# Product-key expert layer and two blocks on one core: dense expert activations for two token tiles instead of three, one tile with gathered u rows, one tile with gathered u and v rows that joins the second block last

## The chip, the cores and the metric

The kernel runs on one core of a Trainium2 chip. The metric is the device time of one execution in microseconds; the kernel before took 2317.34 us (median of three runs, 2315.11 to 2320.51).

## The reference

512 tokens of width 1024 pass through two blocks. The first block has sliding-window attention and a pooling mixer, and then an expert layer with product keys: each token picks, in each of 8 heads, 16 of 16,384 experts. A picked expert has a row in `u_experts` and one in `v_experts`, each of 1024 values. The second block has dilated attention, spatial gating and a gated feed-forward layer. Cut to the expert layer and its surroundings:

```python
def peer(xn, w_query, sub_keys, u_tab, v_tab):      # xn: normed tokens
    def chunk(xc):                                   # 128 tokens
        ...
        sv, si = lax.top_k(sc, PEER_TOPK)            # per head and half: 16 of 128 keys
        ...
        fv, fi = lax.top_k(cand, PEER_TOPK)          # 16 of the 256 pairs
        idx = jnp.take_along_axis(cidx, fi, axis=-1)
        g = jax.nn.softmax(fv, axis=-1)
        u = u_tab[idx]
        a = jax.nn.gelu(jnp.einsum('chkd,cd->chk', u, xc), approximate=False)
        vv = v_tab[idx]
        return jnp.einsum('chk,chkd->cd', (g * a), vv)
...
h = h + peer(rmsnorm(h, ln_ffn_g[l]), ...)
return rmsnorm(h, ln_final_g)                        # then the second block
```

## The kernel before, in words

The 512 tokens are four tiles of 128 (tile 0 to 3). A float32 product is made of three matmuls on split operands (`mm3`, L135): high by high, high by low, low by high. Weights come as 512 KB loads into `wraw` (SyncE's queue), ScalarE copies the high part (`whi`, L130) and VectorE subtracts for the low part (`wlo`, L132).

The expert layer has two ways to serve a tile. **Gathered**: for each of a token's 128 picks an indirect DMA on GpSimd's queue fetches one row per token (128 rows, 512 KB) into one of four `gu` buffers (pool `gt`); for u, VectorE multiplies by the tokens and sums (L466); for v, VectorE adds the scaled row to the residual `hres` (L475). That is 256 gathers for a tile. **Dense**: all 16,384 experts meet the tile on TensorE, in 128 blocks of 128 experts. The activations of a block are 24 matmuls (tile `hps`) over the columns of the dense tiles, then Gelu to `hg`; they are multiplied by a gate matrix that is zero where a token did not pick the expert (`hw`), split (`hh`, `hl`) and multiplied by the block's 128 rows of v, 18 matmuls into six PSUM banks (`acc`). Before, tile 0 is gathered and tiles 1 to 3 are dense, so `hps` has 384 columns (`TD`).

The gate matrix of a tile is built in 8 groups of 16 tokens (`gate_matrix`): VectorE makes `oj` (L596) and part of the `og` (L606), ScalarE the other part (L609, L610), TensorE multiplies them (`wps`, L612), ScalarE copies to `stg` (L614), and 1 MB goes to DRAM. `decode` turns a tile's top-k results into gates and indices, on VectorE. Since the routing leaves TensorE free, `hps` blocks are computed there and **parked** in DRAM: 68 of 128 (`NPARK`), 16 of them beside the queries, the rest by `PARKS` behind each group of the gate matrix. `GATH` sets the gathers per group.

Three lists in the code set the order: within the routing and the second block a scheduler orders each engine's instructions by data and by the order of the code; the dense loop over 128 blocks is written by hand (`manual_schedule`, L695 on): it loads v three blocks ahead, splits two ahead, makes `hw` one ahead, and issues 0.9 gathers a block while activations are parked and 2.5 where they aren't (`RATE`). Engines take their instructions strictly in order, so a VectorE instruction that waits for a gather holds up all behind it.

The second block begins with the last norm of all four tiles and a transposition (`to_feature`), then `token_major` runs `w_in_2` in five column blocks over the four tiles, each weight pair serving all tiles; attention goes by tile (`scores`, `values`) in between.

Of the kernel before, what the change touches and what calls it, by code (L numbers as in the profile page):

```python
# [41 lines left out]
def body(ctx: ExitStack, tc: tile.TileContext, A: dict, out: bass.AP):  # L42
# [31 lines left out]
    def rstd_newton(var, which):  # L74
        """1 / sqrt(var + eps) by three Newton steps from the exponent-halving guess, on the vector engine alone."""
# [24 lines left out]
    def first_half(junk_pool, y):  # L100
        """mean square of a row's first half, halved, plus the norm's eps"""
# [23 lines left out]
    def wload(src, shape):  # L125
# [3 lines left out]
        hi = pool.tile(shape, F32R, name="whi", tag="whi")  # L129
        SC.activation(hi, raw, AF.Copy)  # L130
        lo = pool.tile(shape, F32R, name="wlo", tag="wlo")
# [23 lines left out]
    def halves(mm_pool, srcs, xh, xl, fill, parts=(0, 1)):  # L155
        """The blocks of srcs, two token tiles ahead of the other two; fill() readies those."""
        ws = [wload(src, [128, ND, 128]) for src in srcs]
        pss = [mm_pool.tile([128, S], F32, name="mm", tag="mm") for _ in srcs]
        for part in parts:
            sl = slice(part * 256, part * 256 + 256)  # L160
            if part == parts[1]:
                fill()
# [29 lines left out]
    # ------------------------------------------------ first block: mixers  # L192
# [203 lines left out]
    # ------------------------------------------------ product-key experts  # L396
    # token tile 0 gathers its expert rows; the other tiles meet every expert on the tensor engine
    with ExitStack() as st:
# [4 lines left out]
        gt = st.enter_context(tc.tile_pool(name="gt", bufs=4, reuse_waits="tile"))  # L403
# [3 lines left out]
        TD = S - 128  # L407
        TG = 16
# [688 lines left out]
```

## Time and profile before

| | us |
|---|---|
| median of three runs | 2317.34 |
| span of the profiled execution | 2313.5 |
| queries and top-k, 16 parked blocks (382 to 568.6 of the span) | 186.6 |
| gate matrices, 52 parked blocks, about 59 gathers (568.6 to 897) | 328.4 |
| dense loop (897 to 1690) | 793.0 |
| second block up to its feed-forward part (1690 to 1937) | 247.0 |
| the rest of the second block (1937 to 2313.5) | 376.5 |

The stages follow each other, so a stage's length is its share of the time. In each, the engines' busy times and the busy share of the 16 DMA engines tell which resource has no room left. The busy time of TensorE counts overlapping matmuls; what one costs in a row of its like is the distance between starts.

### The profile page before, as it was taken

The page shows a single profiled execution, that of the slowest core. Times are in us where ns is not written, and L with a number is a line of the kernel's source. Part 1 is how long each engine was busy: PE and PEld are TensorE (multiplying, and loading weights), DVE is VectorE, ACT ScalarE, POOL GpSimd, SP SyncE. Part 2 cuts the span into 40 slices and gives each one's busy share as a digit, 9 for nine tenths or more (in the row PEclk, how much of TensorE's full clock was granted, in tenths as well). Part 3 has the DMA queues.
Part 4 walks back from the last instruction along what each step waited for, and adds up shares of the span by engine and source line. Part 5 has one row for each costly group of instructions (what it writes and reads, how often), then busy time and mean ns, then how long its engine had stood idle before and what let it go on. Part 6 is the DMA issues. An engine that isn't in the chain of part 4 may idle for free.

```text
span 2313.5 us, 30184 instructions
## 1 busy us (share of the span) xinstructions
PE 2246.8 (97%) x11337; PEld 1931.4 (83%) x11337; DVE 1495.2 (65%) x2998; ACT 986.1 (43%) x1631; POOL 382.4 (17%) x261
## 2 busy tenths in 40 slices
PE   7999998999899999999999999999999999999998
PEld 6768887989799999777779999999976778888886
DVE  4553254989999994767777777777784555333323
ACT  4354233333897783333333333333353364322222
POOL 0000000000222430323323444444400000000000
PEclk9999999999899999999999999999999999999999
DMA  5202232443577997889899898889732112333331
GB/s 173 92 19 75 90 111 84 128 125 118 213 272 289 363 350 253 295 311 329 293 323 322 306 320 297 296 302 323 274 113 74 56 55 87 105 101 93 98 100 65
DMA packets 177572, 444.82 MB, mean 192 GB/s; under 512 B 15249, under 2 KB 84241, under 8 KB 174353
## 3 DMA queue, kind: packets, MB, share of 16 engines
q1 hardware_dynamic: 140560, 308.65, 39.8%
q0 software_dynamic: 36864, 134.23, 16.3%
q8 instruction: 89, 1.46, 0.2%
q14 instruction: 59, 0.48, 0.1%
HBM read 402.19 MB, written 40.63 MB: 191 GB/s over the span
## 4 chain that ended last, share of the span: by engine, by line
PE 86%; DVE 5%; ACT 4%; DMA 4%; issue 1%; DVEq 0%; ACTq 0%; SPq 0%
PE mm L136 13%; PE mm L137 12%; PE mm L138 12%; PE hps L138 7%; PE hps L136 7%; PE hps L137 7%; PE acc L136 6%; PE acc L138 6%; PE acc L137 6%; DMA wraw<-in_v_experts_dram 3%; PE wps L612 2%; PE sc L311 1%; PE pv L346 1%; ACT stg L614 1%; PE sc L889 1%
## 5 line engine op out<-in xcount | busy, mean ns | idle before, releaser
L130 ACT ACTIVATE whi<-wraw 128x1024 fp32r<-128x1024 f32 x232 | 241.8, 1045 | 568.9 <-PE mm L137 343.0
L132 DVE TENSOR_TENSOR wlo<-wraw,whi 128x1024 fp32r<-128x1024 f32 x232 | 278.7, 1204 | 265.9 <-ACT whi L130 261.5
L136 PE MATMUL hps<-x2h,whi 128*128 128x384 f32 x1024 | 348.1, 340 | 2.1 <-ACT whi L130 1.8
L138 PE MATMUL hps<-x2h,wlo 128*128 128x384 f32 x1024 | 345.1, 337 | 0.8 <-DVE wlo L132 0.8
L137 PE MATMUL hps<-x2l,whi 128*128 128x384 f32 x1024 | 344.2, 336 | 0.0
L464 POOL DMA_INDIRECT gu<-in_u_experts_dram,ix x128 | 190.8, 1491 | 914.0 <-PE wps L612 605.5
L136 PE MATMUL acc<-whi,hh 128*128 128x512 f32 x768 | 302.6, 394 | 17.3 <-ACT hh L117 17.3
L138 PE MATMUL acc<-whi,hl 128*128 128x512 f32 x768 | 303.2, 395 | 0.0
L137 PE MATMUL acc<-wlo,hh 128*128 128x512 f32 x768 | 302.7, 394 | 0.0
L664 DVE TENSOR_TENSOR wlo<-wraw,whi 128x1024 fp32r<-128x1024 f32 x188 | 227.5, 1223 | 74.6 <-ACT whi L662 69.0
L662 ACT ACTIVATE whi<-wraw 128x1024 fp32r<-128x1024 f32 x188 | 198.3, 1056 | 171.3 <-issue 85.5
L473 POOL DMA_INDIRECT gv<-in_v_experts_dram,ix x128 | 189.7, 1482 | 380.7 <-DVE hres L475 275.3
L136 PEld LDWEIGHTS hps<-x2h,whi 128*128 128x128 f32 x1024 | 193.3, 189 | 5.4 <-ACT whi L130 2.1
L137 PEld LDWEIGHTS hps<-x2l,whi 128*128 128x128 f32 x1024 | 193.1, 189 | 2.7
L138 PEld LDWEIGHTS hps<-x2h,wlo 128*128 128x128 f32 x1024 | 193.1, 189 | 1.1 <-DVE wlo L132 1.1
L136 PEld LDWEIGHTS acc<-whi,hh 128*128 128x128 f32 x768 | 145.5, 189 | 49.6 <-ACT hh L117 21.0
L138 PEld LDWEIGHTS acc<-whi,hl 128*128 128x128 f32 x768 | 145.8, 190 | 33.3 <-DVE hl L118 2.7
L137 PEld LDWEIGHTS acc<-wlo,hh 128*128 128x128 f32 x768 | 145.7, 190 | 29.3
L475 DVE SCALAR_TENSOR_TENSOR hres<-gv,ga,hres 128x1024 f32<-128x1024 f32 x128 | 164.1, 1282 | 1.0
L466 DVE CUSTOM_DVE_ANT_0 gu<-gu,xtok 128x1024 f32<-128x1024 f32 x128 | 154.5, 1222 | 0.0
L137 PE MATMUL mm<-x4l,whi 128*128 128x512 f32 (+1 forms) x384 | 143.9, 375 | 0.0
L136 PE MATMUL mm<-x4h,whi 128*128 128x512 f32 (+1 forms) x384 | 143.3, 376 | 0.3 <-ACT x4h L117 0.3
(316 smaller groups left out, 4022.3 us busy)
## 6 DMA issues: line engine op xcount, KB each, us to landing
wraw<-in_u_cols_dram SPq DMA_DIRECT2D x128, 512.0 KB
wraw<-in_v_experts_dram SPq DMA_DIRECT2D x128, 512.0 KB
wraw<-in_w_in_dram SPq DMA_DIRECT2D x50, 512.0 KB
wdr<-stg SPq DMA_DIRECT2D x24, 1024.0 KB
wt<-wdr SPq DMA_DIRECT2D x16, 1536.0 KB
park<-hg SPq DMA_DIRECT2D x68, 192.0 KB
hg<-park SPq DMA_DIRECT2D x68, 192.0 KB
wraw<-in_w_gate_dram SPq DMA_DIRECT2D x22, 512.0 KB
```

The source lines that it names most:

```text
L130: SC.activation(hi, raw, AF.Copy)
L132: V.tensor_tensor(lo, raw, f(hi), op=OP.subtract)
L136: PE.matmul(ps, lhsT=ah, rhs=bh, start=start, stop=False)
L137: PE.matmul(ps, lhsT=ah, rhs=bl, start=False, stop=False)
L138: PE.matmul(ps, lhsT=al, rhs=bh, start=False, stop=stop)
L464: GP.indirect_dma_start(out=u, out_offset=None, in_=A["u_experts"], in_offset=bass.IndirectOffsetOnAxis(ap=ix[:, s_:s_ + 1], axis=0))
L466: V.tensor_tensor_reduce(out=u, in0=u, in1=xtok, scale=1.0, scalar=0.0, op0=OP.mult, op1=OP.add, accum_out=a[:, s_:s_ + 1])
L473: GP.indirect_dma_start(out=v, out_offset=None, in_=A["v_experts"], in_offset=bass.IndirectOffsetOnAxis(ap=ix[:, s_:s_ + 1], axis=0))
L475: V.scalar_tensor_tensor(hres[:, 0, :], v, a[:, s_:s_ + 1], hres[:, 0, :], op0=OP.mult, op1=OP.add)
L612: PE.matmul(ps[:, k, :], lhsT=oj[:, 4 * e + k, :], rhs=og)
L662: SC.activation(hi, raw, AF.Copy)
L664: V.tensor_tensor(lo, raw, f(hi), op=OP.subtract)
```

## The change

- Tiles 0 and 1 are dense in full; `hps` has 256 columns (`TH`). All 125 blocks behind the first three are parked (`NPARK`), in `park` tiles of 128 KB; the dense loop has only the v part left.
- Tile 2 is dense in v only: its 128 u rows per token are gathered (`gather_half`, 8 per group of the gate matrices of tiles 0 and 1), and its gate matrix, built last, carries gate times activation, not the gate alone. In the dense loop its columns of `hw` are a ScalarE copy.
- Tile 3 is gathered in u and v (`gather_late`): 3 gathers per group of tile 2's gate matrix, 1.35 per dense block, 5 per step of `proj` in the second block. The second block runs tiles 0 to 2 first and takes tile 3 last, reading `w_in_2` a second time for it.
- `gt` has three buffers instead of four. VectorE makes half of the `og` in each tile (before a half, then three quarters); in tile 2 ScalarE needs three instructions for an `og`.

```diff
-NPARK = 68
-NLEAD = 3
-PARKS = ((), (2, 1), (2, 2), (2, 1))
-GATH = (0, 1, 3, 3)
-RATE = (0.9, 2.5)
-DECODE = {(1, 1): 0, (1, 4): 2, (2, 3): 3}
-ON_DVE = ((), (0, 2), (0, 1, 2), (0, 1, 2))
+NLEAD = 3
+NPARK = 128 - NLEAD
+PARKS = (4, 4, 3)
+HALF = 8
+LATE = 3
+TAIL = 5
+RATE = 1.35
+DECODE = {(0, 3): 1, (1, 3): 3}
+ON_DVE = ((0, 2), (0, 2), (0, 2))
...
-        gt = st.enter_context(tc.tile_pool(name="gt", bufs=4, reuse_waits="tile"))
+        gt = later.enter_context(tc.tile_pool(name="gt", bufs=3, side="right", reuse_waits="tile"))
...
-            ps = psh.tile([128, TD], F32, name="hps", tag="hps")
-            fm_block(ps, uh, ul, xh[:, :, 128:], xl[:, :, 128:], ND)
+            ps = psh.tile([128, TH], F32, name="hps", tag="hps")
+            fm_block(ps, uh, ul, xh[:, :, :TH], xl[:, :, :TH], ND)
...
+        def gather_half():
             for h in range(8):
...
+                yield from gather_u(2, h)
+
+        def gather_late():
+            for h in range(8):
+                yield from gather_u(3, h)
                 for s_ in range(16 * h, 16 * h + 16):
                     v = gt.tile([128, D], F32, name="gv", tag="gu")
...
-                spread(parks, 1)
+                spread(parks, 1 + hp_ % 2)
...
+                                if t == 2:
+                                    SC.activation(og, og, AF.Relu, scale=-1.0, bias=1.0)
+                                    SC.activation(og, og, AF.Copy, scale=sT[:, 2, tok:tok + 1])
...
+                spread(parks, PARKS[t])
+                if t < 2:
+                    spread(half, HALF)
+                else:
+                    spread(gathers, LATE)
...
-            for t in range(1, NT):
+            ahead = {t: decode(t) for t in (2, 0)}
+            for t in range(3):
+                if t == 2:
+                    spread(half, 128)
+                    slots(*ahead[2], 2, [ga[2]])
...
+            V.tensor_tensor(hw3[:, :nh, :], hg.rearrange("p (g t) -> p g t", g=nh), wt[:, :nh, n % 8, :], op=OP.mult)
+            SC.activation(hw3[:, nh:, :], wt[:, nh:, n % 8, :], AF.Copy)
...
-                want = int(min(n + 1, 71) * RATE[0] + max(n - 70, 0) * RATE[1])
+                want = int((n + 1) * RATE)
...
             def proj(c, t, ps):
+                if t < 3:
+                    spread(gathers, TAIL)
...
+            got = {2: scores(2)}
+            w_in_2((2,), (0, 1, 2))
             got[1] = scores(1)
+            w_in_2((4,), (0, 1, 2))
             values(2, *got[2])
             got[0] = scores(0)
+            spatial((0, 1, 2))
+            w_in_2((3,), (0, 1, 2))
             values(1, *got[1])
             values(0, *got[0])
...
+            spread(gathers, 256)
+            ready((3,))
...
+            w_in_2((0, 1), (3,))
+            got[3] = scores(3)
+            w_in_2((2, 4), (3,))
...
+            spatial((3,))
+            w_in_2((3,), (3,))
+            values(3, *got[3])
+            half_feature(gv[:, 3, :], 3, 4)
```

**VectorE, one group of a gate matrix.** Before (tile 3's), a group has two `oj`, twelve `og`, two `wlo` of parked blocks and three or four gathers (`ISA gu` is the sum over a gathered row, the line behind it reads the sum out).

```order
L596 TENSOR_TENSOR oj<-io,sT 128x1024
L132 TENSOR_TENSOR wlo<-wraw,whi 128x1024
L466 ISA gu,ga<-gu,xtok 128x1024
L466 ISA ga 128x1
L466 ISA gu,ga<-gu,xtok 128x1024
L466 ISA ga 128x1
L132 TENSOR_TENSOR wlo<-wraw,whi 128x1024
```

Now (tile 0's or 1's), from the end of one group on:

```order
L135 TENSOR_TENSOR wlo<-wraw,whi 128x1024 x3
L475 ISA gu,ga_2818<-gu,xtok_2819 128x1024
L475 ISA ga_2818 128x1
L475 ISA gu,ga_2818<-gu,xtok_2819 128x1024
L475 ISA ga_2818 128x1
L135 TENSOR_TENSOR wlo<-wraw,whi 128x1024
L475 ISA gu,ga_2818<-gu,xtok_2819 128x1024
L475 ISA ga_2818 128x1
L621 TENSOR_TENSOR oj<-io,sT 128x1024
L475 ISA gu,ga_2818<-gu,xtok_2819 128x1024
```

A group now has four `wlo` instead of two and eight gathers instead of three or four; behind these rows come, in this group, one gather, one `og`, one gather, three `og`, `oj`, two gathers and four `og`.

**VectorE, the dense loop.** Before, while activations are parked, one block between a gather (L475) and the next block's `wlo`:

```order
L475 SCALAR_TENSOR_TENSOR hres<-gv,ga,hres 128x1024
L664 TENSOR_TENSOR wlo<-wraw,whi 128x1024
L685 TENSOR_TENSOR hw<-hg,wt 128x384
L118 TENSOR_TENSOR hl<-hw,hh 128x384
L664 TENSOR_TENSOR wlo<-wraw,whi 128x1024
```

Now, one block with two gathers (a block in three has two):

```order
L698 TENSOR_TENSOR wlo<-wraw,whi 128x1024
L475 ISA gu,ga_2822<-gu,xtok_2823 128x1024
L475 ISA ga_2822 128x1
L721 TENSOR_TENSOR hw<-hg,wt 128x256
L120 TENSOR_TENSOR hl<-hw,hh 128x384
L475 ISA gu,ga_2822<-gu,xtok_2823 128x1024
```

`hw` lost a third of its columns on VectorE, and a gather came between `wlo` and `hw`.

**VectorE, the begin of the second block.** Before, norms (L809, L756) and the sums of the dense tiles with `hres`:

```order
L746 TENSOR_TENSOR hres<-hres,acc_8547 128x512
L746 TENSOR_TENSOR hres<-hres,acc_8548 128x512
L91 RECIPROCAL rs<-sd 128x1
L132 TENSOR_TENSOR wlo<-wraw,whi 128x1024
L809 SCALAR_TENSOR_TENSOR hres<-hres,rs,gain 128x1024
```

Now, with the norm's line L848:

```order
L475 ISA gu,ga_2822<-gu,xtok_2823 128x1024
L475 ISA ga_2822 128x1
L781 TENSOR_TENSOR hres<-hres,acc_10933 128x512
L781 TENSOR_TENSOR hres<-hres,acc_10934 128x512
L475 ISA gu,ga_2822<-gu,xtok_2823 128x1024
L475 ISA ga_2822 128x1
L93 RECIPROCAL rs<-sd 128x1
L848 SCALAR_TENSOR_TENSOR hres<-hres,rs,gain 128x1024
```

Gathers of tile 3 stand between the steps of the first norms.

## Rows read from the trace of the kernel before

**Rows 1.** The page's first part: TensorE's busy time, share, instructions
```profile
PE 2246.8 (97%) x11337; PEld 1931.4 (83%) x11337; DVE 1495.2 (65%) x2998; ACT 986.1 (43%) x1631; POOL 382.4 (17%) x261
```
**Rows 2.** Stages: bounds and length; busy PE, PEld, DVE, ACT, POOL; clock, DMA share, GB/s
```profile
568.60:897.00 328.40, 314.12 (x2011) 306.93 (x2011) 299.78 (x576) 258.00 (x477) 84.82 (x59) 0.98 0.80 291
897.00:1690.00 793.00, 775.71 (x3699) 677.96 (x3698) 591.72 (x743) 285.90 (x381) 295.68 (x197) 0.99 0.87 300
898.00:1212.00 314.00, 296.71 (x1279) 242.09 (x1279) 223.19 (x300) 108.93 (x141) 96.13 (x60) 0.98 0.89 303
740.00:820.00 80.00, 79.81 (x530) 78.87 (x529) 79.86 (x146) 60.94 (x111) 34.23 (x25) 1.00 0.98 368
1690.00:1937.00 247.00, 241.07 (x1146) 180.22 (x1144) 143.01 (x373) 120.53 (x239) 1.68 (x1) 1.00 0.24 77
```
**Rows 3.** Timeline of TensorE: start, length of single matmuls with 384 and 256 columns
```profile
876.00 0.33 PE L138 MATMUL hps<-x2h,wlo 128*128 128x384 f32 x1
...
884.84 0.33 PE L138 MATMUL hps<-x2h,wlo 128*128 128x384 f32 x1
...
1939.12 0.41 PE L136 MATMUL mm<-x4h,whi 128*128 128x256 f32 x1
1939.33 0.41 PE L137 MATMUL mm<-x4l,whi 128*128 128x256 f32 x1
...
1945.00 0.28 PE L138 MATMUL mm<-x4h,wlo 128*128 128x256 f32 x1
...
1950.40 0.28 PE L136 MATMUL mm<-x4h,whi 128*128 128x256 f32 x1
```
**Rows 4.** Groups by line: busy us, mean ns of one | idle before, releaser
```profile
L132 DVE TENSOR_TENSOR wlo<-wraw,whi 128x1024 fp32r<-128x1024 f32 x224 | 273.2, 1222 | 262.1 <-ACT whi L130 257.7 <-ACT hg L450 1.4
L606 DVE TENSOR_SCALAR og<-io,sT 128x128 f32<-128x128 f32 x256 | 72.0, 354 | 5.2 <-PE wps L612 3.9 <-PE hps L138 1.3
L614 ACT ACTIVATE stg<-wps 128x512 f32<-128x512 f32 x96 | 101.9, 1079 | 2.5 <-PE wps L612 2.5
L610 ACT ACTIVATE og<-og,sT,nT 128x128 f32<-128x128 f32 x128 | 58.2, 488 | 0.5
L609 ACT ACTIVATE og<-io,nT 128x128 f32<-128x128 f32 x128 | 46.2, 395 | 0.0
```
**Rows 5.** DMA queues over the whole span, then over 898 to 1212: packets, MB, share
```profile
q0 software_dynamic: 36864, 134.23, 16.3%
...
q1 hardware_dynamic: 47547, 63.83, 62.0%
```
**Rows 6.** Timelines of GpSimd and VectorE at gathers; q0's packets in 1075.0 to 1078.6
```profile
606.04 1.08 POOL L464 DMA_INDIRECT gu<-in_u_experts_dram,ix  x1 [605.53 <-PE wps L612]
...
610.93 1.22 DVE L466 CUSTOM_DVE_ANT_0 gu<-gu,xtok 128x1024 f32<-128x1024 f32 x1
...
1071.42 1.80 POOL L473 DMA_INDIRECT gv<-in_v_experts_dram,ix  x1 [2.28 <-DVE hres L475]
...
q0 software_dynamic: 144, 0.52, 36.6%
```
**Rows 7.** The chain that ended last: start, length, what
```profile
575.26 4.40 DVE eq L560 x2
...
751.45 3.57 PE wps L612 x32
...
936.48 12.63 DMA wraw<-in_v_experts_dram
```
**Rows 8.** Timeline of VectorE over one block of the dense loop
```profile
1069.87 1.28 DVE L475 SCALAR_TENSOR_TENSOR hres<-gv,ga,hres 128x1024 f32<-128x1024 f32 x1
1071.18 1.22 DVE L664 TENSOR_TENSOR wlo<-wraw,whi 128x1024 fp32r<-128x1024 f32 x1
...
1073.47 0.56 DVE L118 TENSOR_TENSOR hl<-hw,hh 128x384 fp32r<-128x384 f32 x1 [0.59 <-ACT hh L117]
1073.94 1.28 DVE L475 SCALAR_TENSOR_TENSOR hres<-gv,ga,hres 128x1024 f32<-128x1024 f32 x1
```

More of the change, by code (lines that the diff above doesn't have):

```diff
@@ L128, in wload @@
         SY.dma_start(raw, src)
-        hi = pool.tile(shape, F32R, name="whi", tag="whi")
+        pool, th, tl = place or (pool, "whi", "wlo")
+        hi = pool.tile(shape, F32R, name="whi", tag=th)
         SC.activation(hi, raw, AF.Copy)
-        lo = pool.tile(shape, F32R, name="wlo", tag="wlo")
+        lo = pool.tile(shape, F32R, name="wlo", tag=tl)
         V.tensor_tensor(lo, raw, f(hi), op=OP.subtract)
@@ L407, in body @@
         TD = S - 128
+        TH = 256
         TG = 16
@@ L479, in body @@
         parks = park_blocks()
-        gathers = gather_steps()
+        half = gather_half()
+        gathers = gather_late()
         def spread(gen, n):
@@ L741, in body @@
                         mm3(acc[t][c], hh[:, sl], hl[:, sl], vh[:, cs], vl[:, cs], False, n == 127)
-            spread(gathers, 256)
         for t in range(3):
@@ L745, in body @@
                 cs = slice(c * 512, (c + 1) * 512)
-                V.tensor_tensor(hres[:, t + 1, cs], hres[:, t + 1, cs], acc[t][c], op=OP.add)
+                V.tensor_tensor(hres[:, t, cs], hres[:, t, cs], acc[t][c], op=OP.add)
     with ExitStack() as st:
-        wps.append(st.enter_context(tc.tile_pool(name="wpc", bufs=4, reuse_waits="tile")))
+        wps.append(st.enter_context(tc.tile_pool(name="wpc", bufs=3, reuse_waits="tile")))
         def xs_norm(wk, t, g):
@@ L797, in body, with of3, ready @@
             SC.activation(cos[:, :, 0, :], ang, AF.Sin)
-            xh = ft.tile([128, ND, S], F32R, name="x3h", tag="xh")
-            xl = ft.tile([128, ND, S], F32R, name="x3l", tag="xl")
-            with tc.tile_pool(name="wkx", bufs=2, reuse_waits="tile") as wkx:
+            x3h = ft.tile([128, ND, S - 128], F32R, name="x3h", tag="x3h")
+            x3l = ft.tile([128, ND, S - 128], F32R, name="x3l", tag="x3l")
+            def of3(x):
+                return lambda k, sl: x[:, k, sl.start % 384:(sl.stop - 1) % 384 + 1]
+            def ready(tiles):
                 gfin = gain("ln_final_g")
@@ L847, in proj @@
                 elif c == 3:
-                    SC.activation(gu[:, t, :], ps, AF.Gelu)
-                    V.tensor_tensor(gu[:, t, :], gu[:, t, :], gv[:, t, :], op=OP.mult)
-                    half_feature(gu[:, t, :], t, 4)
+                    gu = wk.tile([128, 512], F32, name="gu2")
+                    SC.activation(gu, ps, AF.Gelu)
+                    V.tensor_tensor(gv[:, t, :], gu, gv[:, t, :], op=OP.mult)
                 else:
@@ L861, in proj, with w_in_2 @@
                     V.tensor_tensor(y, y, gln[:, 512:], op=OP.add)
-            token_major([pmm] * 4, "w_in_2", (0, 1), ND, whole(xh), whole(xl), proj, lead=2)
+            def w_in_2(cols, tiles, **kw):
+                token_major([pmm] * 4, "w_in_2", cols, ND, of3(x3h), of3(x3l), proj, order=tiles, **kw)
+            w_in_2((0, 1), (0, 1, 2), lead=2)
             ch = [ft.tile([128, 4, S], F32R, name="ca")]
@@ L919, in values, with spatial @@
                 half_feature(o, t, 0)
-            def spatial():
+            def spatial(tiles):
                 for g in range(8):
```

162 lines of the change are left out of this document (88 added, 74 removed).

## The prediction, made before the changed kernel was run

> **What bounds the kernel now.** I read the page's engine shares first, then the stages by windows, then rows of single instructions. TensorE is busy for 97% of the span [rows 1], which suggests that cutting its work shortens the kernel. The stages say less [rows 2]: in the gate-matrix stage VectorE is busy 299.8 of 328.4 us, and in its densest part, 740 to 820, VectorE is busy 79.9 of 80 us while the DMA engines are at 98% and move 368 GB/s. Three resources end together there. In the first part of the dense loop the DMA share is 0.89 and TensorE has gaps. One block there takes VectorE 4.07 us from gather to gather [rows 8], which is also 18 matmuls at 0.226 us. So two of the stages that the change touches have no free DMA and little free VectorE; only the second block has (DMA share 0.24, VectorE busy 143 of 247 us).
>
> **What it removes.** The `hps` matmuls shrink from 384 to 256 columns. Starts lie 8.84 us apart over 51 steps, 0.173 us each, and 5.40 us over 45 steps, 0.120 us [rows 3]. 128 blocks of 24 matmuls at 0.053 us less are 164 us of TensorE, a gain only where TensorE sets the pace.
>
> **What it adds.** 128 more indirect DMAs (384 instead of 256). One costs all 16 engines 16.3% of 2313.5 us / 256 = 1.47 us [rows 5]: 189 us of DMA. Each also has a VectorE instruction of 1.2 to 1.3 us [rows 6, 8], together 166 us. The rest adds 20 weight loads in the second block.
>
> The DMA sum first, for the gate stage and the dense loop together. Before: 0.80 x 328.4 + 0.87 x 793 = 953 us [rows 2]. Add 189; take off the 60 gathers that go to the second block (88); add some 18 for more parked tiles (125 of 128 KB, written and read, are 32.8 MB instead of 26.7; q1 takes 0.62 x 314 / 63.83 = 3.05 us per MB [rows 5]); take off 11 for eight u loads that move to the queries. That is 1060 us at a share of 1, where both stages now take 1121. At 0.86, about the present share, it is 1230 us. TensorE's 164 us can't be had there.
>
> **Queries.** 24 parked blocks instead of 16: 24 x 2.88 against 16 x 4.16 us of TensorE, +3 us.
>
> **Gate stage.** A group of tile 0 or 1 has, per resource:
> - TensorE: 4 x 24 x 0.120 + 3.6 (32 `wps` [rows 7]) = 15.1 us.
> - VectorE: 4 `wlo` x 1.22, 8 gathers x 1.30 (with the read-out), 2 `oj` like a `wlo`, 8 `og` x 0.28 (72.0 / 256) [rows 4, 6] = 19.9 us.
> - ScalarE: four `whi` and Gelu pairs at about 1.4, 8 `og` x 0.82, 4 `stg` x 1.06 [rows 4] = 16.4 us.
> - DMA: 12 x 0.524 + 1.05 + 4 x 0.131 = 7.86 MB at 368 GB/s [rows 2] = 21.4 us.
>
> To this comes the gather's loop, with three buffers: a buffer is asked for again when VectorE has read it. At the first gather 4.9 us pass from issue to use; at a busy one all 144 packets lie 3.6 to 7.2 us behind the issue; a v load waits up to 12.6 us [rows 6, 7]. I take 7, near the busy gather's row, bounds 4.9 and 12.6. Walking the new VectorE order with that, gather 4 waits about 2 us for the buffer of gather 1, gathers 6 and 7 about 1 each, and VectorE with everything behind it (`og`, `wlo`, so TensorE's work) waits too: 23.6 us a group at 6.8, 26.0 at 8. I take 24.5; 16 groups are 392 us. Before, with four buffers and three gathers in 12 us, this loop was hidden.
>
> In front, two decodes instead of one: some 12 us of VectorE each (4.4 us of it the first `eq` [rows 7]), 30 us with the filling. Two more inside the groups, partly in the waits: 18. Tile 2's groups have three ScalarE instructions for half of the tokens: 8 x 1.18 + 4.2 + 3 x 1.4 = 17.8 us [rows 4] against 12.2 on TensorE and DMA: 8 groups, 150 us with waits. Its gates need the last gathered activation (4), and five parked blocks remain (14). Sum 30 + 392 + 18 + 150 + 4 + 14 = 608 us, **+280** against 328.4. Bounds: 21.4 a group, 540 us; 30 a group, 700 us.
>
> **Dense loop.** TensorE needs 4.07 us a block. VectorE: 1.34 gathers x 1.31, `wlo` 1.14, `hw` with its wait for ScalarE 1.0 instead of 1.15, `hl` 0.47 [rows 8] = 4.4 us. DMA: eight blocks before took 37 us at 0.89 = 32.9 us; 3.6 more gathers add 5.2 and the smaller `hg` saves 1.6: 36.5, or 4.56 us a block. At a share of 0.94, between 0.89 and the 0.98 of the densest window [rows 2], 4.85 us. 128 x 4.85 + 9 for the first three blocks = 630 us, **-163**; bounds 604 and 660. The u loads and their splits, which filled the second part of this loop, are what is saved; they were moved into the gate stage, where +280 pays for them.
>
> **Second block.** 60 gathers come in. VectorE has some 145 us of work up to the last of them (60 x 1.3, the splits, norms and rotations), and their loop needs at least 60 x (4.9 + 1.3) / 3 = 124 us [rows 6]; TensorE has about 110 us of work there. I take +40 (bounds 10 and 70). Then tile 3 goes alone: norms and transposition with nothing beside them 9 us, 20 weight loads at some 1.6 us for 1.37 us of matmuls each 5, and the waits of rotation, gating norm and last `half_feature`, which three other tiles covered before, 11. Together **+65**; bounds 20 and 110. The rest is unchanged.
>
> **Sum.** 2313.5 + 3 + 280 - 163 + 65 = 2498.5 us of span. The median stood 3.8 us over the profiled span; I predict **2502 us**.
>
> **Two rules weighed.** The gather at 1071.4 landed 7 us after its issue [rows 6]. The Trainium skill, "DMA: Bandwidth & Descriptors", section on the anatomy of one DMA on the GpSimd path, gives about 2.0 us plus the bytes at 436 GB/s, for 512 KB an estimate of 3.2 us. By it three buffers would hide the loop, the groups would take the DMA's 21.4 us and the time would be some 50 us less; the row disagrees, since queues are full here. A second rule bears on the third rival below.
>
> **Rivals.**
> 1. *DMA runs full through both stages.* Some reordering by the queues lets the 1060 us of DMA go through at 0.98: 1081 us, -40; gathers in the second block hide behind matmuls and tile 3 alone costs 20. 2313.5 - 40 + 3 + 20 + 3.8 = 2300 us, faster. For it: 0.98 over 80 us [rows 2]. Against it: tile 2's groups are bound by ScalarE at a DMA share of about 0.65, and the decodes move next to nothing. It decides from a mean share of 0.965 up. Chance 0.06.
> 2. *No waits for buffers.* Groups at 21.4 us (gate stage 540), the loop at 4.65 us a block (604), second block +40: 2313.5 + 3 + 212 - 189 + 40 + 3.8 = 2383 us. For it: the first gather's 4.9 us. Against it: that one ran with empty queues. Chance 0.12.
> 3. *The loop of a gather is longer.* At 10 us a gather takes (10 + 1.3) / 3 = 3.8 us whatever VectorE does: 30 us a group, +90; 5.06 us a dense block, +27; second block +35: 2654 us. For it: the v loads' 12.6 us [rows 7]. Chance 0.12. GpSimd's issues last 1.08 us at the first gather and 1.80 at the busy one [rows 6]; if every issue were held for one more VectorE instruction, the loop would be 8.2 us plus reading, nearly 27 us a group. The Trainium skill, "SBUF — State Buffer", section on the two sides of SBUF, says that VectorE in some modes locks GpSimd out of the port through which it writes descriptors. No run here shows which of these instructions would do it.
>
> TensorE's clock is no rival of its own: after the pause before 1937 matmuls of 256 columns started 0.21 us apart, later 0.120 [rows 3], half the clock against full. A group would then need 4 x 24 x 0.213 + 3.6 = 24 us, still under 24.5.
>
> **How the numbers follow.** The forecast has 0.70, the rivals 0.06, 0.12 and 0.12. The range **2370 to 2610** takes in the second rival and the forecast's bounds (a group at 22 to 28 us is -40 and +56, the loop -26 and +30, the second block -45 and +45; not all at one end). Left out are the first and third rivals, 0.18. A difference of 0.2%, 4.6 us, is about what can be told from no change: faster 0.06, the same 0.03, slower 0.91.
>
> **What would show it.** Right: groups of tile 0 and 1 near 24 us with TensorE under two thirds busy and VectorE waiting for `gu`; tile 2's groups near 18 us with ScalarE nearly full; a dense loop near 630 us without `hps`, at a DMA share over 0.9; a second block near 312 us with TensorE waiting until the gathers end. Wrong: TensorE near full in the gate stage, or a gate stage under 500 us; a dense loop near 530 us, which would mean that DMA carries more than the rows say; gathers that leave no trace in the second block.

## The result, and the profile after

The changed kernel takes **2560.72 us** (median of four runs, 2556.31 to 2571.15) against 2318.38 us for the kernel before on the same chip (four runs, 2315.11 to 2320.51): a ratio of 1.106, 95% interval 1.103 to 1.108. The forecast was 2502 us, its range 2370 to 2610. The profiled execution has a span of 2554.6 us, 6.1 us under the median.

The page's first part and the releasing chain of the kernel after, to be held against [rows 1]:

```profile
PE 2220.8 (87%) x11353; PEld 1852.4 (73%) x11353; DVE 1632.4 (64%) x3220; ACT 1081.9 (42%) x1996; POOL 547.6 (21%) x389
...
PE 50%; DMA 18%; DVE 12%; issue 11%; ACT 4%; POOL 4%; SPq 1%; DVEq 0%; POOLq 0%; ACTq 0%
...
q0 software_dynamic: 55296, 201.35, 22.5%
```

TensorE fell from 97% of the span to 87%: the columns saved in `hps` came back as idle time, not as a shorter span. The gathers' queue, q0, carries 201 MB instead of 134 [rows 5].

The stages of the kernel after (bounds and length; busy PE, PEld, DVE, ACT, POOL; TensorE's granted clock, DMA share, GB/s). They answer to [rows 2]; the second and third line are the groups of tiles 0 and 1 and those of tile 2 within the first:

```profile
571.00:1194.50 623.50, 465.84 (x3226) 447.11 (x3225) 456.12 (x776) 372.83 (x774) 234.43 (x155) 0.82 0.80 280
615.00:1034.00 419.00, 299.87 (x1984) 287.68 (x1983) 302.13 (x506) 232.08 (x452) 182.97 (x118) 0.78 0.81 283
1071.00:1170.00 99.00, 89.27 (x697) 86.30 (x696) 79.39 (x122) 93.77 (x234) 27.23 (x21) 0.95 0.91 323
1194.50:1841.00 646.50, 571.48 (x2334) 445.76 (x2332) 478.47 (x656) 228.16 (x396) 248.40 (x174) 0.95 0.91 311
1841.00:2171.70 330.70, 259.27 (x1121) 191.25 (x1121) 231.90 (x475) 151.38 (x275) 64.58 (x57) 0.87 0.56 180
2171.70:2554.60 382.90, 372.81 (x1697) 306.94 (x1696) 126.03 (x145) 106.92 (x146) 0.00 (x0) 0.99 0.29 88
```

| stage, us | before | forecast | after | after minus forecast |
|---|---|---|---|---|
| queries | 186.6 | 189.6 | 189.0 | -0.6 |
| gate matrices | 328.4 | 608 | 623.5 | +15.5 |
| dense loop | 793.0 | 630 | 646.5 | +16.5 |
| second block to its feed-forward part | 247.0 | 312 | 330.7 | +18.7 |
| the rest | 376.5 | 376.5 | 382.9 | +6.4 |
| median less span | 3.8 | 3.8 | 6.1 | +2.3 |

The line between the last two stages of the expert layer was drawn at 1690 before, 8.5 us ahead of the last `acc` step (1698.5), and is at 1841 after, just behind it (1839.9). The forecast so counted 8.5 us twice, in the loop's 630 and in the 247 to which it added 65. From the last `acc` step on, the second block took 239 us before and takes 332 after: +93, not +65.

In the groups of tiles 0 and 1 (second line) no engine is full, and the DMA engines aren't either: TensorE 72%, VectorE 72%, DMA 81%. Waits that follow on each other fill the rest. One group shows them. VectorE in the kernel after, from 753.49 on (start, length; in brackets the idle time before it and what ended it):

```profile
753.49 1.23 DVE L475 CUSTOM_DVE_ANT_0 gu<-gu,xtok 128x1024 f32<-128x1024 f32 x1
...
756.31 1.23 DVE L135 TENSOR_TENSOR wlo<-wraw,whi 128x1024 fp32r<-128x1024 f32 x1 [1.59 <-ACT whi L133]
760.26 1.23 DVE L475 CUSTOM_DVE_ANT_0 gu<-gu,xtok 128x1024 f32<-128x1024 f32 x1 [2.73 <-DMA gu<-in_u_experts_dram,ix]
...
765.30 1.23 DVE L475 CUSTOM_DVE_ANT_0 gu<-gu,xtok 128x1024 f32<-128x1024 f32 x1 [1.49 <-DMA gu<-in_u_experts_dram,ix]
...
769.97 1.23 DVE L475 CUSTOM_DVE_ANT_0 gu<-gu,xtok 128x1024 f32<-128x1024 f32 x1 [3.17 <-DMA gu<-in_u_experts_dram,ix]
...
776.36 3.48 DVE L135 TENSOR_TENSOR wlo<-wraw,whi 128x1024 fp32r<-128x1024 f32 x3
```

Three waits for gathered rows, 7.4 us in all, in a group of 27 us. They fall on the group's third, fifth and sixth gather; the walk in the prediction had some 2 us for gather 4 and 1 each for 6 and 7. GpSimd at the same time (the row waited for at 760.26 is that of the issue at 748.94, counted in order):

```profile
746.96 1.68 POOL L473 DMA_INDIRECT gu<-in_u_experts_dram,ix  x1 [2.12 <-DVE ga L475]
748.94 5.27 POOL L473 DMA_INDIRECT gu<-in_u_experts_dram,ix  x1 [0.30 <-DVE og L631]
...
764.08 0.94 POOL L473 DMA_INDIRECT gu<-in_u_experts_dram,ix  x1 [0.64 <-DVE ga L475]
...
776.52 4.16 POOL L473 DMA_INDIRECT gu<-in_u_experts_dram,ix  x1 [0.30 <-DVE og L631]
```

An issue lasts 0.94 us, 1.68 us when it starts in a single sum over a row, and 4.16 us when it starts with the three `wlo` in a row at 776.36: it ends 0.84 us after they do. The one of 5.27 us lies beside three `wlo` and the sum behind them. Before, the busy one was 1.80 us [rows 6]. Of 134 issues between 571 and 1071, 11 last over 4 us; they are called held from here on.

### The profile page after: what moved, and what is told of

The parts are those of the page before. It is cut to its first block, busy times and chain, and to the rows that moved or that the text cites. A ratio compares the mean times of both kernels' runs of the same rounds, so it can differ in the third digit from the quotient of the medians.

```text
span 2554.6 us, 31606 instructions
## 1 busy us (share of the span) xinstructions
PE 2220.8 (87%) x11353; PEld 1852.4 (73%) x11353; DVE 1632.4 (64%) x3220; ACT 1081.9 (42%) x1996; POOL 547.6 (21%) x389
## 4 chain that ended last, share of the span: by engine, by line
PE 50%; DMA 18%; DVE 12%; issue 11%; ACT 4%; POOL 4%; SPq 1%; DVEq 0%; POOLq 0%; ACTq 0%
PE mm L140 10%; PE mm L139 10%; PE mm L141 10%; DMA wraw<-in_v_experts_dram 7%; DMA gu<-in_u_experts_dram,ix 7%; POOL gu L473 4%; PE acc L139 3%; PE acc L141 3%; DVE gu L475 3%; PE acc L140 3%; DMA gv<-in_v_experts_dram,ix 2%; ACT whi L696 2%; DVE wlo L698 2%; DVE hres L492 1%; PE sc L314 1%
## 5 line engine op out<-in xcount | busy, mean ns | idle before, releaser
L473 POOL DMA_INDIRECT gu<-in_u_experts_dram,ix x256 | 378.8, 1480 | 1113.0 <-ACT nT L614 587.2
L133 ACT ACTIVATE whi<-wraw 128x1024 fp32r<-128x1024 f32 (+1 forms) x309 | 323.1, 1047 | 650.5 <-PE mm L140 271.5
L135 DVE TENSOR_TENSOR wlo<-wraw,whi 128x1024 fp32r<-128x1024 f32 (+1 forms) x309 | 370.1, 1207 | 307.2 <-ACT whi L133 304.9
L475 DVE CUSTOM_DVE_ANT_0 gu<-gu,xtok 128x1024 f32<-128x1024 f32 x256 | 311.0, 1225 | 126.3 <-DMA gu<-in_u_experts_dram,ix 126.0
L139 PE MATMUL hps<-x2h,whi 128*128 128x256 f32 x1024 | 308.7, 301 | 31.4 <-ACT whi L133 14.4
L141 PE MATMUL hps<-x2h,wlo 128*128 128x256 f32 x1024 | 297.4, 294 | 11.1 <-DVE wlo L135 11.1
L140 PE MATMUL hps<-x2l,whi 128*128 128x256 f32 x1024 | 300.6, 294 | 0.0
L641 PE MATMUL wps<-og,oj 128*128 128x128 f32 x768 | 147.3, 360 | 105.1 <-DVE og L631 93.6
L698 DVE TENSOR_TENSOR wlo<-wraw,whi 128x1024 fp32r<-128x1024 f32 x131 | 160.2, 1223 | 80.1 <-ACT whi L696 76.9
L696 ACT ACTIVATE whi<-wraw 128x1024 fp32r<-128x1024 f32 x131 | 138.3, 1056 | 142.6 <-PE acc L141 78.0
```

The source lines that it names most:

```text
L135: V.tensor_tensor(lo, raw, f(hi), op=OP.subtract)
L139: PE.matmul(ps, lhsT=ah, rhs=bh, start=start, stop=False)
L140: PE.matmul(ps, lhsT=ah, rhs=bl, start=False, stop=False)
L141: PE.matmul(ps, lhsT=al, rhs=bh, start=False, stop=stop)
L473: GP.indirect_dma_start(out=u, out_offset=None, in_=A["u_experts"], in_offset=bass.IndirectOffsetOnAxis(ap=ix[t][:, s_:s_ + 1], axis=0))
L475: V.tensor_tensor_reduce(out=u, in0=u, in1=xtok[t], scale=1.0, scalar=0.0, op0=OP.mult, op1=OP.add, accum_out=a[:, s_:s_ + 1])
```

## The experiments

Two theories stand for the groups of tiles 0 and 1, which the expectations name by a word. **LOOP**: three buffers, each asked for again only when VectorE has read it, so that VectorE waits for gathers. **LOCK**: GpSimd's issues are held while VectorE runs instructions with two inputs in SBUF, and the gathers come late for that. Beside them stand the engines and the DMA queues as plain bounds. The table has the median (one run where no interval is given), the time from the first to the sixteenth store of `stg` (15 groups of tiles 0 and 1), the dense loop from the first to the last `acc` step, and from there to the first feed-forward matmul.

| kernel | us | interval of the ratio | 15 groups | dense loop | second block |
|---|---|---|---|---|---|
| after | 2560.7 | 1.103 to 1.108 | 418.2 | 637.7 | 331.8 |
| e1, six buffers | 2528.3 | 1.088 to 1.094 | 393.7 | 645.2 | 336.3 |
| e2, four buffers | 2534.3 | 1.092 to 1.097 | 400.2 | 656.9 | 330.4 |
| e3, one input | 2530.0 | | 391.5 | 641.6 | 336.0 |
| e4, 384 columns | 2633.5 | | 433.5 | 641.9 | 331.9 |
| e5, no fetch | 2442.6 | | 280.8 | 648.8 | 337.5 |
| e6, no sum | 2465.7 | | 343.2 | 645.7 | 328.6 |
| e7, all before | 2614.6 | | 420.2 | 738.6 | 285.3 |
| e8, no late gathers | 2397.2 | | 417.4 | 527.5 | 283.8 |
| e9, more late | 2522.7 | 1.089 to 1.094 | 388.3 | 577.8 | 399.9 |
| e10, four and five | 2517.8 | 1.086 to 1.089 | 386.6 | 658.2 | 328.5 |
| e11, one input, padded | 2551.3 | 1.100 to 1.107 | 405.6 | 649.2 | 325.9 |

**More buffers (e1, e2).**

```diff
+        g2 = mix.enter_context(tc.tile_pool(name="g2", bufs=3, side="right", reuse_waits="tile"))
-                u = gt.tile([128, D], F32, name="gu", tag="gu")
+                u = (g2 if t == 2 and s_ % 2 else gt).tile([128, D], F32, name="gu", tag="gu")
```

> Tile 2's 128 u gathers alternate between the three buffers of the pool gt and three more of their own, so six buffers instead of three while the gate matrices of tiles 0 and 1 are built; the rest is the changed kernel. Theory LOOP (three buffers make VectorE wait 126 us for gu): a group of tile 0 or 1 falls from 27.3 us to the DMA engines' 21.4 or a little over, about 23, and the time by 16 x 4.3 = 70 us to about 2490. Rival LOCK (GpSimd's issue is held while VectorE runs instructions with two SBUF inputs: 11 of 134 issues took 4 to 5.3 us): more buffers let GpSimd run ahead, so that the held issues are hidden too, and the saving is the same; it is told apart by e3. Rival DMA (the engines set the pace, share 0.83 in these groups): under 20 us less.

e2 gives `gt` a fourth buffer for all gathers, and takes one of two `pt` buffers away:

> Pool gt with four buffers as in the kernel before, for all gathers; to make room, the attention's pt tile has one buffer instead of two. LOOP: groups at about 24.5 us (minus 45), the second block's gathers at (4.9 + 1.3) / 4 = 1.6 us instead of 2.1 (minus 15 to 25), the dense loop unchanged: about 2495. DMA: under 20 us less. The single pt buffer may cost the second block some us.

e1 took 32 us off, e2 26. Between the two no difference is shown: their intervals overlap. The waits between 571 and 1034 (engine, line, releaser: us in total, times, longest), of the kernel after and then of e1:

```profile
DVE gu L475 <- DMA gu<-in_u_experts_dram,ix: 95.4, 52, 4.0
ACT whi L133 <- DMA wraw<-in_u_cols_dram: 74.6, 30, 6.4
```
```profile
ACT whi L133 <- DMA wraw<-in_u_cols_dram: 120.7, 44, 6.3
DVE wlo L135 <- ACT whi L133: 57.0, 20, 5.0
```

The 95 us of waits for rows are gone from e1's list (3.3 us are left), but only 24.5 us of the 418 went with them: ScalarE now waits longer for weight loads (115.4 us up to 1010, where e1's groups of tiles 0 and 1 end), and VectorE behind it for `whi`. The waits that LOOP names are real, and they are a smaller part than I expected.

The held issues went as well: of the 140 issues between 571 and 1071, in e1 and in e2, none lasts over 2.7 us. Three `wlo` still stand in a row in 15 places in either, but no issue starts in such a row any more. So the 32 and 26 us are the price of both theories together, and e1 and e2 don't tell them apart.

**Held issues (e3, e11).** In e3 the low part of a parked block's weights comes from an instruction with one input (the subtraction is left out):

```diff
-            uh, ul = wload(A["u_cols"][n], [128, ND, 128])
+            uh, ul = wload(A["u_cols"][n], [128, ND, 128], "one")
...
+        if one:
+            V.tensor_scalar(lo, raw, eps[:, 0:1], eps[:, 1:2], op0=OP.mult, op1=OP.mult)
+            return hi, lo
```

> In the parked blocks VectorE's wlo (two inputs from SBUF) is an instruction of the same 1024 columns with one SBUF input and two scalars per partition; the subtraction for the low part of the u weights is left out there. LOCK: no issue of an indirect DMA in the groups of tiles 0 and 1 takes over 2.1 us (now 11 of 134 take 4 to 5.3), gathers are issued up to 3 us earlier once per group, groups fall by 1.5 to 3 us, the time by 25 to 45 us. LOOP alone: the time falls by the shorter instruction only, 4 x 0.1 us a group, under 10 us in all.

-31 us, and of 142 issues between 571 and 1071 none lasts 4 us (three last over the 2.1 us of the text, the longest 3.02): nearly as LOCK expects. But the instruction was also shorter, and didn't wait for ScalarE. The line in e3:

```profile
L137 DVE TENSOR_SCALAR wlo<-wraw,eps x125: 758/806/893, 392.9 to 1148.2; 128x1024 fp32r<-128x1024 f32 x125
```

0.81 us where the `wlo` has 1.22 [rows 4]. So e11 gave it its wait and its length back:

```diff
-            V.tensor_scalar(lo, raw, eps[:, 0:1], eps[:, 1:2], op0=OP.mult, op1=OP.mult)
+            V.tensor_scalar(lo, f(hi), eps[:, 0:1], eps[:, 1:2], op0=OP.mult, op1=OP.mult)
+            V.tensor_scalar(lo[:, :5], raw[:, :5], eps[:, 0:1], eps[:, 1:2], op0=OP.mult, op1=OP.mult)
```

> As e3, but of VectorE's old length: in e3 the instruction in place of a parked block's wlo took 0.81 us (1.22 before) and didn't wait for ScalarE's copy, so that its -31 us could be VectorE's time (4 x 0.4 us in 16 groups are 26 us) and not GpSimd's held issues. Here two one-input instructions stand for one wlo, the first reading whi, so that it waits as the wlo did, the second reading 5/8 of wraw; together about 1.2 us. The subtraction is left out. After: 2561 us. If held issues are the cause, issues stay under 2 us as in e3, and so does the gain: 2530 to 2540 us. If VectorE's time was the cause, issues are short, too, and the gain is gone: 2550 to 2565 us.

2551.3 us: most of e3's gain is gone, while the issues stay short (137 in that stretch, mean 1.23 us, none over 3). The lines of its two instructions follow. Where they stand in a row, two of the first took 1.54 us and two of the second 1.12, so a pair takes 1.33 us, against 1.16 for a `wlo` in a row (3.48 / 3):

```profile
L137 DVE TENSOR_SCALAR wlo<-whi,eps x125: 764/808/997, 392.5 to 1170.0; 128x1024 fp32r<-128x1024 f32 x125
L138 DVE TENSOR_SCALAR wlo<-wraw,eps x125: 593/607/685, 394.6 to 1170.9; 128x640 fp32r<-128x640 f32 x125
```

The intervals of e11 and after overlap. With the padding up to 0.17 us too long in 64 places, 11 us, the held issues are worth between nothing and some 20 us here. Without e11 I would have put down 31 us to LOCK. What e3 took away besides is 0.4 us of VectorE four times a group, 26 us over 16 groups, and VectorE's waits for `whi` (22.8 us between 571 and 1034 in the changed kernel); the 15 groups fell by 26.7 us, though VectorE idles 28% there. e11 gives both back together, so which of the two counted isn't shown.

Held issues aren't needed for the waits for rows either: e11 has none, and up to 1023, where its groups of tiles 0 and 1 end, VectorE still waits 88.4 us for rows.

**TensorE (e4).** `hps` in parked blocks at 384 columns again (the result's last 128 are not used):

```diff
-            ps = psh.tile([128, TH], F32, name="hps", tag="hps")
-            fm_block(ps, uh, ul, xh[:, :, :TH], xl[:, :, :TH], ND)
+            ps = psh.tile([128, TD], F32, name="hps", tag="hps")
+            fm_block(ps, uh, ul, xh[:, :, :TD], xl[:, :, :TD], ND)
```

> The parked blocks' activations are computed on TensorE for 384 columns as before (tile 2's 128 columns are not used), all else is the changed kernel: TensorE's 24 x 125 x 0.053 = 160 us of work come back without any DMA or VectorE work. If TensorE sets no pace behind the queries (my theory): plus 24 x 1.28 = 31 us in the queries, where TensorE is full, and under 40 us in the gate stage, so 2560 to 2630; if TensorE were the bound of the gate stage too: plus 160, to 2720.

+73 us, just over the 2630 of the first forecast, of which 27 are in the queries (the first store at 642.9 instead of 615.5) and 25 in tile 2's groups (122.6 us for seven instead of 97.6). In the 15 groups of tiles 0 and 1, where 60 blocks of 24 matmuls at 0.053 us are 76 us more of TensorE at full clock, 15 us came out. TensorE is not their bound. (Its granted clock there rose from 0.78 to 0.88, so its busy time rose by 53 us only, from 299 to 352.) In the other two places the addition came out nearly whole (24 and 21 blocks of 1.27 us are 31 and 27 us): there TensorE has next to no room.

**What the gather costs, and what its sum costs (e5, e6).** e5 leaves the fetch of tile 2's u rows out and sums over a constant buffer; e6 (with e1's six buffers) keeps the fetch and puts a product of one column in the sum's place.

```diff
                 if t == 2:
                     V.tensor_tensor_reduce(out=uo, in0=ub, in1=xtok[t], scale=1.0, scalar=0.0,
                                            op0=OP.mult, op1=OP.add, accum_out=a[:, s_:s_ + 1])
                     yield
                     continue
```

> Tile 2's 128 u rows per token are not fetched: each sum runs over a resident buffer of constants (VectorE's instruction stays). Left out: 128 of 384 gathers. With six buffers a group of tiles 0 and 1 still took 24.5 to 25 us; this run and the next ask what that is. A group has 15.9 us of VectorE-independent DMA less 8 x 1.47 = 11.8 us: DMA about 10 us, VectorE 19.9 us, TensorE 15.1 us. If the fetch (its DMA, its buffers, its issues beside VectorE) holds the group: 20.5 us a group, 16 x 6.5 = 104 us off, 2455 us. If VectorE's order and the waits among VectorE, ScalarE and TensorE hold it: 24.5 us a group, the buffers' part alone comes off, 2525 us.

```diff
                 if t == 2:
                     V.tensor_tensor(a[:, s_:s_ + 1], u[:, 0:1], xtok[t][:, 0:1], op=OP.mult)
```

> Six buffers as in e1, and the sum over a gathered u row of tile 2 is replaced by a product of one column (the gather stays; the activations of tile 2 are not computed). VectorE falls to about 9.5 us a group. To be compared with e1 (2528 us). If DMA sets the group (21.4 us at 368 GB/s, 24.5 at the share of 0.81 to 0.85 seen): 24 us a group, within 15 us of e1, 2515 us. If VectorE sets it: the next limit is DMA at its best, 21.5 us, 16 x 3.2 = 50 us off, 2478 us.

Either removal brought the larger gain that its text names, and some: 2442.6 us (2455 if the fetch holds the group) and 2465.7 us (2478 if VectorE does). The stretch from 615 to 862 in e5, and then in e6:

```profile
615.00:862.00 247.00, 224.94 (x1762) 217.98 (x1763) 230.58 (x393) 197.55 (x396) 8.20 (x3) 0.96 0.62 208
```
```profile
615.00:862.00 247.00, 193.11 (x1424) 185.92 (x1423) 137.13 (x308) 162.46 (x320) 122.27 (x105) 0.90 0.99 389
```

Without the fetch VectorE is 93% busy (18.7 us a group, decodes included); without the sum the DMA engines are 99% busy at 389 GB/s (22.9 us a group). So the groups have two limits close to one another, and the kernel runs at neither: 27.9 us after, 26.2 with six buffers. My reading is that the work takes turns on them, since a load waits for a buffer that VectorE frees and VectorE for a load. It would also explain why e3's gain is as large as the time it took off VectorE. The two limits are shown, the turns are argued.

**Are the loads late for want of buffers? (e10)** Four buffers for the u rows of tile 2, five for the weights of parked blocks:

```diff
+        if hasattr(place, "tile"):
+            raw, place = place.tile(shape, F32, name="wraw", tag="wraw", bufs=2), None
...
+        g2 = mix.enter_context(tc.tile_pool(name="g2", bufs=1, side="right", reuse_waits="tile"))
-            uh, ul = wload(A["u_cols"][n], [128, ND, 128])
+            uh, ul = wload(A["u_cols"][n], [128, ND, 128], g2 if n % 2 else None)
-                u = gt.tile([128, D], F32, name="gu", tag="gu")
+                u = (g2 if t == 2 and s_ % 4 == 3 else gt).tile([128, D], F32, name="gu", tag="gu")
```

> Four buffers for the gathered u rows of tile 2 and five instead of three for the loads of the parked blocks' weights. Nothing is left out. In e1 ScalarE waits 83.3 us of 247 us for loads of u_cols, and no longer VectorE for gathered rows. To be compared with e2 (four buffers everywhere, 2534 us, 25 us a group). If the loads come late because three buffers don't cover their time of landing: 22.5 us a group, 16 x 2.5 = 40 us off, 2494 us. If they come late because the DMA engines are shared with the gathers: 24.5 to 25 us a group, within 12 us of e2.

-16.5 us against e2, between the two forecasts and nearer to the shared queues. The waits between 571 and 1034 in e10:

```profile
DVE gu L479 <- DMA gu<-in_u_experts_dram,ix: 90.2, 56, 4.1
ACT whi L136 <- DMA wraw<-in_u_cols_dram: 67.4, 27, 5.2
```

In e2 the same two waits are 52.6 us for rows and 125.0 for weights. The wait for weights went down to 67 us and the wait for rows came back to 90, with no held issue (the longest is 2.6 us). The gathers did not take longer for it: from the issue of a row that VectorE waited for to its use it is 7.9 us on average in e10, and 8.2 in e2. So VectorE came to its rows sooner instead; what holds the rest stays open. It is the fastest form of the changed kernel that leaves nothing out, and still 8.8% slower than before.

**Dense loop and second block (e7, e8, e9).** e7 changes `RATE` to 1.85, so that all late gathers end before the second block; e8 leaves the 172 gathers of the loop and the 60 of the second block out; e9 has six buffers, `RATE = 1.0` and `TAIL = 7`.

```diff
-RATE = 1.35
+RATE = 1.85
```

> 1.85 gathers a dense block instead of 1.35: all gathers of tile 3 end before the second block. Nothing is left out. Dense loop: 60 gathers x 1.47 us of DMA at the share of 0.91 are 97 us more, 744 us instead of 646. Second block up to the feed-forward part, 331 us now: if the late gathers set most of its 84 us over before's 247 (forecast 40 of 65), it falls by 60 to 272 us and the time is 2597 us; if tile 3 going alone sets them, it falls by 20 and the time is 2637 us.

```diff
-RATE = 1.35
+RATE = 0.0
...
-                if t < 3:
-                    spread(gathers, TAIL)
...
-            spread(gathers, 256)
```

> The 172 gathers of the dense loop and the 60 of the second block are left out (tile 3's expert sum is then incomplete); tile 3 still goes alone, last. Dense loop: if DMA sets its pace, the share times the time is 0.91 x 5.05 = 4.6 us a block now and 2.6 without the gathers, so TensorE's 18 matmuls, 4.07 us, set it: 535 us instead of 646. If something else in the loop (splits, hw, waits between engines) sets it: over 600 us. Second block: 272 us if the gathers set most of the addition (time 2390 us); 312 us if tile 3 alone does (2430 us).

Without its gathers the loop takes 527.5 us, at which TensorE is busy 524.7 of 528 us: the first line below, e8's windows. The second is e7's loop, where 60 more gathers cost 101 us, 1.68 us each, near the 97 us expected. The whole of e7, 2614.6 us, lies between its two forecasts. The last two are the second block in e7 and in e8:

```profile
1203.00:1731.00 528.00, 524.72 (x2305) 431.51 (x2305) 273.86 (x386) 227.80 (x382) 1.09 (x1) 1.00 0.64 204
```
```profile
1207.00:1945.00 738.00, 600.11 (x2300) 441.48 (x2299) 544.57 (x736) 219.21 (x389) 298.47 (x230) 0.94 0.88 309
1946.00:2230.00 284.00, 246.47 (x1119) 182.18 (x1119) 163.04 (x388) 148.09 (x271) 0.00 (x0) 0.93 0.33 106
```
```profile
1731.00:2014.00 283.00, 247.58 (x1121) 183.00 (x1120) 163.54 (x388) 148.30 (x271) 0.00 (x0) 0.93 0.33 106
```

The second block takes 284 to 285 us in both, with no gather in it: of the 93 us that it grew in the changed kernel, the 60 gathers are 47, and the new order with tile 3 alone at its end is 46.

> Six buffers as in e1 (2528 us), and 1.0 gathers a dense block instead of 1.35, 7 a step in the second block instead of 5: 44 gathers move from the dense loop to the second block. Nothing is left out. Dense loop: by e7, 60 gathers cost it 100.6 us, 1.68 each, so 44 fewer are worth 74: 645 down to 571 (TensorE's floor there is 527, from e8). Second block: by e7, 60 gathers cost it 47 us, 0.78 each. If that price holds, +34, in all -40: 2488 us. If the room beside its matmuls is used up with 60, the next 44 cost their whole loop of three buffers, (4.9 + 1.3) / 3 = 2.1 each, +91, in all +17: 2545 us.

e9 gave 2522.7 us, between the two and not to be told from e1 (6 us less, the intervals overlap): the loop fell by 67 us (44 gathers, 1.53 each) and the second block grew by 64 (1.44 each). The first 60 gathers cost 0.78 us each there; the room beside the second block's work was mostly used up by them.

## Why the prediction was right, and where it was off

The direction, the mechanism and the order of the stages' sizes held; the sum was 59 us short, and each term below is one that was mis-sized.

**The two DMA sums held.** The forecast was 1060 us at a share of 1 for gate stage and dense loop; measured are 0.80 x 623.5 + 0.91 x 646.5 = 1087 us. The mean share is 0.86, as assumed for both stages together. This is what excludes the first rival: it needed 0.965, and e6 reached 0.99 only in one stretch, with VectorE's work taken away.

**Groups of tiles 0 and 1: 24.5 us forecast, 26.9 measured** where they run evenly (701.31 to 889.51, seven groups, by the stores below). The issues of the gathers in this stretch (duration min, median, max in ns; then from issue to landing), and VectorE's waits:

```profile
L473 POOL DMA_INDIRECT gu<-in_u_experts_dram,ix x56: 932/939/5272, 701.5 to 885.3; - x56
...
DMA to landing us min/median/max: 4.2/6.9/12.0
```
```profile
DVE gu L475 <- DMA gu<-in_u_experts_dram,ix: 47.0, 22, 4.0
DVE wlo L135 <- ACT whi L133: 12.1, 7, 1.9
```

The price of one turn was right in the middle: 7 us taken, 6.9 measured. The error was to walk the group with one value for every gather, where the landings spread from 4.2 to 12.0 us, and VectorE waits for the late ones: 6.7 us a group instead of 4. The wait for `whi`, 1.7 us a group, was put at nothing. VectorE's own work was 18.4 us a group instead of 19.9 (129.0 us in seven), which hid part of the error. Six of the rows waited for came from held issues and account for 17.2 of the 47.0 us. The second rival (21.4 us) is out; the third (30 us) was the nearer of the two. The 27 us that its text names if every issue is held are met in number only: seven of these 56 issues last over 4 us, and the median landing is 6.9 us, not 8.2.

The two groups with a decode took 41.0 and 41.7 us, 31 us over two plain ones (25.8 on average over the other 13) where 18 were forecast.

Stores of `stg` by SyncE in the kernel after: three of tile 0, then three of tile 2:

```profile
725.99 0.32 SPq L644 DMA_DIRECT2D wdr<-stg  x1
753.49 0.32 SPq L644 DMA_DIRECT2D wdr<-stg  x1
780.74 0.32 SPq L644 DMA_DIRECT2D wdr<-stg  x1
...
1071.77 0.33 SPq L644 DMA_DIRECT2D wdr<-stg  x1
1083.68 0.33 SPq L644 DMA_DIRECT2D wdr<-stg  x1
1097.10 0.32 SPq L644 DMA_DIRECT2D wdr<-stg  x1
```

**Tile 2's groups: 18.75 us forecast, 13.9 measured** (97.6 us for seven), an error to the other side of 34 us. The bound that was named, ScalarE, is the busiest engine (93.8 of 99 us); that it alone is the bound isn't shown, since TensorE is busy 89.3 us there and DMA at 0.91, and no run took work off ScalarE. Its work was oversized: the 17.8 us added up the busy times of groups of instructions in [rows 4], each group by itself (1.18 us for an `og` of three instructions), and on ScalarE neighbours of different groups overlap, too. In tile 2's seven groups the busy times by line add up to 115 us, and ScalarE was busy for 92.4 of the 97.6 us. Two instructions in a row in tile 2 (each 0.39 and 0.31 us alone):

```profile
1096.86 0.66 ACT L634 ACTIVATE og<-io,nT 128x128 f32<-128x128 f32 x2
1097.41 0.51 ACT L636 ACTIVATE og<-og 128x128 f32<-128x128 f32 x2
1097.82 0.69 ACT L637 ACTIVATE og<-og,sT 128x128 f32<-128x128 f32 x2
```

Two take 0.66 us, not 0.78, and the next kind starts 0.11 us before they end. The distance between starts is the price, and I used it for TensorE and not for ScalarE. That the gate stage came out only 15.5 us off is so in part by luck: +17 in plain groups, +16 in the two with a decode, -34 in tile 2's; the way from the last of tile 1 to the first store of tile 2 took 38.1 us instead of 22.75 (+15), the trailing parks 25 instead of 14 (+11), the begin 44.5 instead of 54.5 (-10).

**Dense loop: 630 forecast, 646.5 measured.** That the gathers set its pace, e7 and e8 show from both sides, and buffers aren't their price here (656.9 us with four in e2). That it is their DMA, as I had said, and not VectorE's part of them rests on the shares (DMA 0.91, VectorE busy 478 of 646 us); no run takes the two apart. The work of DMA per block was right; the share was 0.91 and not 0.94: at 0.91 the 621 us of the 128 blocks are 641, with the 9 of the first blocks 650. I had taken a value between the 0.89 of the loop before and the 0.98 of the densest window; the lower row was the nearer one.

**Second block: 312 forecast, 330.7 measured.** From the last `acc` step it is +93 instead of +65: the 60 gathers 47 instead of 40, tile 3 alone 46 instead of 25 (which of norms, weight steps and attention cost more than I had added up wasn't separated), less the 8.5 us that the forecast had counted twice. The two parts of the stage after, up to about the end of the last gather and from there:

```profile
1840.40:2000.00 159.60, 112.46 (x441) 79.64 (x440) 128.43 (x260) 58.54 (x101) 65.18 (x57) 0.83 0.73 240
2000.00:2171.70 171.70, 147.17 (x684) 111.61 (x683) 103.47 (x216) 93.05 (x174) 0.00 (x0) 0.90 0.40 126
```

TensorE works 112.5 of 159.6 us and VectorE 128.4 while gathers run, against the 110 and 145 us of the forecast; after that TensorE works 147 of 172 us.

**The rest: 0 forecast, +6.4 measured.** The feed-forward matmuls are the same in number and lie further apart: those of 512 columns start 0.233 us from one another on average instead of 0.227, some 960 times, which is 6 us. One of their lines before and after (duration min, median, max in ns, and first and last start):

```profile
L136 PE MATMUL mm<-x4h,whi x384: 276/389/582, 1937.5 to 2184.4; 128*128 128x512 f32 x160, 128*128 128x256 f32 x32
```
```profile
L139 PE MATMUL mm<-x4h,whi x384: 279/392/579, 2171.7 to 2425.5; 128*128 128x512 f32 x160, 128*128 128x256 f32 x32
```

From the first to the last start they take 253.8 us instead of 246.9, with one pause of 3.5 us in either and the granted clock at 1.0 in both from 20 us after their begin. The changed kernel has `x4h` in another place of SBUF (`x4` stands at the right side); whether that is the cause wasn't tried and stays open.

**TensorE's clock** was at 0.78 of full over the groups of tiles 0 and 1, a mixture of the two levels (2.4 and 1.2 GHz), where [rows 2] has 0.98: the chain of `wps`, `hps` and pauses that VectorE's waits leave. As forecast, it does not set the pace by itself: e4 put 53 us more of TensorE's busy time there, at a clock of 0.88, and 15 came out. What the lower clock costs beside the waits no run shows.

**The signs.** Two of those named beforehand failed: TensorE was busy 73% of the even groups and not under two thirds, at a granted clock of 0.76, and tile 2's groups took 13.9 us and not near 18. The others held: VectorE waiting for `gu`, a dense loop near 630 us at a share over 0.9, and TensorE idle while the second block's gathers run.

**The two rules weighed.** By the price of the Trainium skill's "DMA: Bandwidth & Descriptors" (section on the anatomy of one DMA on the GpSimd path), an estimate of 3.2 us a gather, three buffers would have hidden the loop. The runs disagree, as the row before did: the median gather landed after 6.9 us, and a fourth to sixth buffer was worth 26 to 32 us, the held issues' part included. The Trainium skill's "SBUF — State Buffer" (section on the two sides of SBUF) says that VectorE and GpSimd share a pair of ports, and that a VectorE instruction with two inputs in SBUF can hold it for its whole length against a GpSimd instruction that reads SBUF. That agrees with the issues of 4.16 and 5.27 us beside three `wlo` in a row and with e11's lack of them. What held issues would make of the time was the third rival; e11 puts that at 20 us or less. VectorE's waits for held rows, ten of them between 571 and 1034, add up to 27.8 us, more than that; in e11 other rows were waited for instead.

## What to carry to other kernels

Work taken from TensorE is worth little in a stage that DMA and VectorE fill: sum the bytes of the stages that a change touches and divide by the share that they reach now, before counting columns. Where two limits lie within some 20% of one another and feed each other through buffers, expect a time above both: here 22.9 us (DMA), 18.7 (VectorE) and 26 to 28 together, and a fourth buffer gives back only a part. An experiment that takes one suspect away has to leave the instruction's length and its waits as they were: e3 alone would have blamed the held issues for what was VectorE's time and its wait. And it is worth looking whether an edit took away more than it was meant to: the extra buffers of e1 and e2 removed the held issues, too.

## What the runs showed of the hardware that was not expected

- An indirect DMA's issue on GpSimd lasts 0.94 us beside an idle VectorE, 1.68 us when it starts in a single VectorE instruction with two SBUF inputs, and 4.16 to 5.27 us when it starts 0.16 us into a row of them without a gap. Where it starts as early in a row of one-input instructions it lasts 1.48 us (e11) and 1.49 us (e3).
- Short ScalarE instructions in a row overlap: two `og` of 0.39 us take 0.66 us.
- Gathers of 128 rows (512 KB) among weight loads and stores landed 4.2 to 12.0 us after their issue, with a median of 6.9 us, at a DMA share of 0.82.
- The same 512-column matmuls of the feed-forward part start 0.227 us apart before and 0.233 us after, at a granted clock of 1.0 in both; the cause is open.
- With VectorE's sums out of the way the DMA engines moved 389 GB/s over 247 us at a share of 0.99 (e6), more than the 368 GB/s of the densest window before [rows 2].
